# Mixer of a hybrid encoder layer: recurrences and in-projections emitted in alternation

## Chip, cores and metric

One core of a Trainium2 chip runs the whole kernel in one launch. The metric is device time in microseconds (us): the median of several executions. TensorE (PE) does the matmuls, VectorE (DVE), ScalarE (ACT) and GpSimd (POOL) the arithmetic around them, SyncE (SP) issues most DMAs.

## The reference

One layer of a streaming encoder: 2048 tokens, width 1024, float32. What the change touches is the mixer:

```python
proj = x @ w_in                                   # one in-projection
mq, mk, mv, mo, mi, mf, gq, gk, gv, gg, glr = split(proj)
mq, mk = split(silu(causal_conv(concat(mq, mk))))
hm = mlstm_chunkwise(mq, mk, mv, i_pre, f_pre)    # 4 heads, C_t = f C_{t-1} + i v k^T
m_out = sigmoid(mo) * head_layer_norm(hm)
log_a = log_sigmoid(glr @ g_lr_w + g_lr_b) / 16
hg = gla_chunked(gq, gk, gv, log_a)               # 4 heads, S_t = diag(a_t) S_{t-1} + k v^T
g_out = silu(gg) * head_rms_norm(hg)
mixed = concat(m_out, g_out) @ w_out
```

A layer norm, cross-attention into 256 memory tokens, a squared-ReLU MLP and further norms follow. Both recurrences carry a state along the tokens, so within a head one chunk needs the state of the chunk before.

## The kernel before

The mixer's work is cut into 24 units, `units` at L827: for each of the six head groups (mLSTM heads 0 and 1, GLA pairs 0 and 1, mLSTM heads 2 and 3) four token blocks of 512. A unit has two halves. The first is dense: `inproj(u)` (L831) calls `m_inproj` or `g_inproj`, which multiply the block's 1024 input features by the head's weights. Float32 precision is made from pairs of float16 values, high and low, so each product is three matmuls: `mm3`, L170 to L172. `inproj_fm` gives one group of 24 matmuls of 512 columns into one PSUM buffer of `mm` (two buffers), `inproj_tm` two groups of 48 matmuls of 256 columns in two halves each. An mLSTM unit has 48 of 512 and 96 of 256, a GLA unit 48 and 192.

The second half is the recurrence, `rec(u)` at L841. For an mLSTM unit, `m_pre` (L419) makes decay weights (`mb`, `scb`), the products of queries and keys (L433) and transposed keys (L439), and `m_rec` (L445) goes through four chunks of 128 tokens: L455 and L457 give the output, L460 the state's product, L465 on DVE the new state `C`. For a GLA unit, `g_gate` (L564) makes the cumulated gates two units ahead, and `g_rec` (L583) builds the masked product of queries and keys from seven levels of block width (64 down to 1). For each level DVE and POOL take differences of gates (L596, L597), ACT the exponential (L598), DVE and POOL multiply (L599, L600), ACT and DVE split into `lxh` and `lxl` (L603, L604), PE does 24 matmuls of 64 columns into `s` (four buffers), and DVE copies the result under a mask (L613). A diagonal (L617 to L624), the decays, transposes of the keys and four chunks (L651 to L663) follow.

The loop over units (L886 to L917) emits for each u: `g_gate(u + 2)`, `m_pre(u)`, `rec(u)`, then `inproj(u + 3)` whole (`LOOK = 3`; three in-projections stand before the loop), and in the first units parts of the cross-attention's weight products (`x_w`, `x_a`, `x_b`). A framework's scheduler then orders each engine's instructions, by the order of emission and its own estimate of when each is ready; every engine executes its own list in order. The gate arithmetic of all mLSTM heads (`gate_math`, ending at L412) stands just before the loop. After the loop the first two output tiles of the mixer, `s1(0)` and `s1(1)` (L807), multiply by `w_out`. Weights come by DMA into one staging buffer each, are scanned for their maximum (L114) and split by ACT (L147) and DVE (L148).

## Time and profile before

| | |
|---|---|
| median of 3 runs | 3002.34 us (3002.3 to 3006.09) |
| the profiled execution | 3002.87 us, its span 3001.0 us |
| TensorE's mean granted clock in it | 0.951 of full |
| busy: TensorE, VectorE, ScalarE, GpSimd | 2738.2, 1991.3, 1096.3, 447.6 us |

Times on the trace count from the span's start. The loop over units runs from about 247 us to 1200 us; what follows is the output products, the cross-attention and the MLP. A granted clock of 1.00 is 2.4 GHz, 0.50 is 1.2 GHz, and a value between is a mean over a stretch with both. A wait is listed as the engine and line that waited, an arrow, and the engine, buffer and line that ended the wait.

### The profile page before, as it was taken

The page shows a single profiled execution, that of the slowest core. Times are in us where ns is not written, and L with a number is a line of the kernel's source. Part 1 is how long each engine was busy: PE and PEld are TensorE (multiplying, and loading weights), DVE is VectorE, ACT ScalarE, POOL GpSimd, SP SyncE. Part 2 cuts the span into 40 slices and gives each one's busy share as a digit, 9 for nine tenths or more (in the row PEclk, how much of TensorE's full clock was granted, in tenths as well). Part 3 has the DMA queues.
Part 4 walks back from the last instruction along what each step waited for, and adds up shares of the span by engine and source line. Part 5 has one row for each costly group of instructions (what it writes and reads, how often), then busy time and mean ns, then how long its engine had stood idle before and what let it go on. Part 6 is the DMA issues. An engine that isn't in the chain of part 4 may idle for free.

```text
span 3001.0 us, 41124 instructions
## 1 busy us (share of the span) xinstructions
PE 2738.2 (91%) x16282; PEld 1545.8 (52%) x16282; DVE 1991.3 (66%) x3774; ACT 1096.3 (37%) x1715; POOL 447.6 (15%) x573
## 2 busy tenths in 40 slices
PE   3679989989998898999999779999999999999997
PEld 2346667666665665565565334444444444444443
DVE  8956774655768666676666467777776676555547
ACT  3335444434444543233223254444443222222230
POOL 1102113322433221121111110000000000000003
PEclk8789999988989999999999889999999999999999
DMA  7832331010001335344435963333345522122211
GB/s 240 240 118 86 106 97 38 20 42 9 23 26 62 98 120 128 66 133 106 109 102 134 175 216 142 134 134 134 134 146 141 194 90 109 67 77 78 78 53 57
DMA packets 276993, 319.51 MB, mean 106 GB/s; under 512 B 200944, under 2 KB 217856, under 8 KB 268096
## 3 DMA queue, kind: packets, MB, share of 16 engines
q1 hardware_dynamic: 268096, 285.43, 31.3%
q0 software_dynamic: 8704, 31.46, 2.9%
q8 instruction: 127, 2.08, 0.3%
q14 instruction: 66, 0.54, 0.1%
HBM read 165.58 MB, written 102.96 MB: 89 GB/s over the span
## 4 chain that ended last, share of the span: by engine, by line
PE 67%; DVE 15%; issue 7%; POOL 4%; ACT 3%; DMA 2%; SPq 2%; POOLq 0%; ACTq 0%; DVEq 0%
PE s L170 9%; PE s L171 9%; PE s L172 9%; PE mm L170 9%; PE mm L172 8%; PE mm L171 8%; PE o L172 4%; PE o L170 4%; PE o L171 4%; SPq L222 2%; DVE wmx L114 1%; DVE qk L334 1%; DVE wlo L148 1%; DVE st L199 1%; PE o L651 1%
## 5 line engine op out<-in xcount | busy, mean ns | idle before, releaser
L1245 DVE SCALAR_TENSOR_TENSOR slab<-s,uiv,slab 128x512 f32<-128x512 f32 x384 | 285.5, 748 | 99.0 <-PE s L172 97.5
L170 PE MATMUL mm<-whi,slab 128*128 128x256 f16 x1024 | 280.3, 274 | 12.4 <-ACT whi L147 7.2
L171 PEld LDWEIGHTS <-whi 128*128 128x128 f16 x1680 | 167.1, 99 | 238.8 <-issue 70.6
L171 PE MATMUL mm<-wlo,slab 128*128 128x256 f16 x1024 | 280.3, 274 | 2.7 <-DVE wlo L148 2.7
L172 PE MATMUL mm<-whi,slab 128*128 128x256 f16 x1024 | 280.3, 274 | 0.0
L172 PEld LDWEIGHTS <-wlo 128*128 128x128 f16 x1936 | 191.9, 99 | 168.4 <-issue 12.6
L170 PEld LDWEIGHTS <-whi 128*128 128x128 f16 x1680 | 167.0, 99 | 198.0 <-issue 13.8
L171 PE MATMUL s<-w,ua 128*128 128x512 f16 x512 | 194.0, 379 | 1.8 <-DVE w L148 1.8
L170 PE MATMUL s<-w,ua 128*128 128x512 f16 x512 | 194.0, 379 | 0.0
L172 PE MATMUL s<-w,ua 128*128 128x512 f16 x512 | 194.0, 379 | 0.0
L172 PE MATMUL o<-slab,wlo 128*128 128x256 f16 (+1 forms) x640 | 189.1, 295 | 0.0
L170 PE MATMUL s<-w,ub 128*128 128x512 f16 x480 | 182.6, 380 | 2.9 <-DVE r L1245 2.9
L171 PE MATMUL s<-w,ub 128*128 128x512 f16 x480 | 182.6, 380 | 0.0
L172 PE MATMUL s<-w,ub 128*128 128x512 f16 x480 | 182.4, 380 | 0.0
L170 PE MATMUL mm<-slab,whi 128*128 128x512 f16 x448 | 178.4, 398 | 0.4 <-ACT sg L343 0.4
L171 PE MATMUL mm<-slab,whi 128*128 128x512 f16 x448 | 178.4, 398 | 0.0
L172 PE MATMUL mm<-slab,wlo 128*128 128x512 f16 x448 | 178.1, 397 | 0.0
L170 PE MATMUL mm<-hf,whi 128*128 128x512 f16 x384 | 146.4, 381 | 11.5 <-ACT slab L1142 11.5
L171 PE MATMUL mm<-hf,whi 128*128 128x512 f16 x384 | 146.3, 381 | 0.0
L172 PE MATMUL mm<-hf,wlo 128*128 128x512 f16 x384 | 146.3, 381 | 0.0
L170 PEld LDWEIGHTS <-slab 128*128 128x128 f16 x1104 | 109.3, 99 | 64.8 <-issue 23.2
L170 PE MATMUL o<-slab,wlo 128*128 128x256 f16 x512 | 139.7, 273 | 0.0
(423 smaller groups left out, 6296.8 us busy)
## 6 DMA issues: line engine op xcount, KB each, us to landing
stg<-in_w_ff SPq DMA_DIRECT2D x17, 1024.0 KB
w_d<-w SPq DMA_DIRECT2D x32, 512.0 KB
slab<-in_w_ff SPq DMA_DIRECT2D x15, 1024.0 KB
w<-w_d SPq DMA_DIRECT2D x30, 512.0 KB
stg<-in_w_x SPq DMA_DIRECT2D x14, 1024.0 KB
stg<-in_w_mix SPq DMA_DIRECT2D x14, 1024.0 KB
h_d<-hs POOLq DMA_DIRECT2D x24, 512.0 KB, 3.8
x<-in_x SPq DMA_DIRECT2D x16, 512.0 KB
```

Source lines behind the costliest of these rows:

```text
L114: nc.vector.tensor_reduce(dst, src, axis=AX.X, op=ALU.max, apply_absolute_value=True)
L148: nc.vector.scalar_tensor_tensor(lo, stg, s, hi, ALU.mult, ALU.subtract)
L170: nc.tensor.matmul(psum, lhsT=lh, rhs=rh, start=(start and i == 0), stop=False)
L171: nc.tensor.matmul(psum, lhsT=lh, rhs=rl, start=False, stop=False)
L172: nc.tensor.matmul(psum, lhsT=ll, rhs=rh, start=False, stop=(stop and i == n - 1))
L199: nc.vector.bn_stats(st[:, i, :], x[:, i * 512:(i + 1) * 512])
L222: nc.sync.dma_start_transpose(dst, src)
L334: nc.vector.scalar_tensor_tensor(cv, raw[:, t:t + TB], cj[:, t:t + 1], cv, ALU.mult, ALU.add)
L651: nc.tensor.matmul(po[j][:, c], lhsT=ATb[j][:, c], rhs=vs[j][:, c], start=True, stop=(S is None))
L1245: nc.vector.scalar_tensor_tensor(acc[ii][:, ns], po, iv, acc[ii][:, ns], ALU.mult, ALU.add)
```

## The change

The functions that emit dense work (`inproj_fm`, `inproj_tm`, `m_inproj`, `g_inproj`) become generators that pause after each half group: 12 matmuls of 512 columns or 24 of 256. `m_pre`, `m_rec` and `g_rec` pause after each step: a level, the diagonal, a chunk and so on. The loop takes a step of `rec(u)`, then one half group of `inproj(u + 2)` (in the first five units also a piece of the cross-attention's products), and so on in turn. So the look-ahead is two units and no longer three; `inproj(2)` moves from before the gate arithmetic into the loop; `m_pre(u + 1)` is emitted inside `rec(u)`; a GLA level's factors are emitted two levels ahead (`prep_level`, with three `lx` buffers for four); the scaled queries are written into `q` in place; `s1(0)` and `s1(1)` are emitted in unit 22. Dense work that is left when a recurrence has ended follows it.

```diff
@@ -295,4 +295,7 @@
             hi, lo = (t.rearrange("p (k n) -> p k n", k=KC) for t in w)
-            mm3(pq, [(hi[:, k, n0:n0 + P], lo[:, k, n0:n0 + P], hT[b][:, :, 0, k, :], hT[b][:, :, 1, k, :])
-                     for k in range(KC)])
+            for k0 in (0, KC // 2):
+                mm3(pq, [(hi[:, k, n0:n0 + P], lo[:, k, n0:n0 + P], hT[b][:, :, 0, k, :], hT[b][:, :, 1, k, :])
+                         for k in range(k0, k0 + KC // 2)], k0 == 0, k0 > 0)
+                if k0 == 0:
+                    yield
             nc.scalar.activation(dst, pq, AF.Copy, scale=scale)
@@ -307,3 +310,6 @@
                         [(hT[b][:, i, 0, k, :], hT[b][:, i, 1, k, :], hi[:, k, :], lo[:, k, :]) for k in range(KC)])
+                    if v == 0:
+                        yield
                 cb(u, pv.rearrange("p (i n) -> p i n", i=2))
+                yield
 
@@ -322,3 +328,3 @@
                 raw = wk.tile([P, 3 + TB], F32, name="raw", bufs=2)
-                inproj_fm(b, (qh, ql), j * P, raw[:, 3:3 + TB], qv)
+                yield from inproj_fm(b, (qh, ql), j * P, raw[:, 3:3 + TB], qv)
                 if b == 0:
@@ -336,2 +342,3 @@
                 qk.append(cv)
+                yield
             v1 = wk.tile([P, CPB, P + 1], F32, name="v1", bufs=3)
@@ -343,3 +350,3 @@
                 nc.scalar.activation(sg[:, u * 2:u * 2 + 2, :], pv[:, :, P:2 * P], AF.Sigmoid, scale=vv)
-            inproj_tm(b, (vh, vl), cb)
+            yield from inproj_tm(b, (vh, vl), cb)
             nc.gpsimd.tensor_tensor(sg, sg, mng[:, h * P:(h + 1) * P].unsqueeze(1).broadcast_to([P, CPB, P]), ALU.mult)
@@ -429,3 +436,3 @@
                 nc.scalar.activation(mb[:, c], mb[:, c], AF.Exp, bias=gcols["c"][:, g0 + c:g0 + c + 1])
-            nc.gpsimd.tensor_tensor(scb, scb, q, ALU.mult)
+            yield
             pS = ps_s()
@@ -436,2 +443,4 @@
                                            mb.rearrange("p c t -> p (c t)"), ALU.mult, ALU.mult)
+            nc.gpsimd.tensor_tensor(q, q, scb, ALU.mult)
+            yield
             pk = ps_s()
@@ -442,3 +451,3 @@
                                     gcols["wj"][:, g0:g0 + 4].unsqueeze(2).broadcast_to([P, CPB, P]), ALU.mult)
-            mpre[u] = mb, scb, kw
+            mpre[u] = mb, q, kw
 
@@ -446,2 +455,5 @@
             q, k, v1, sg = blk
+            nxt = m_pre(u + 1) if u + 1 < len(units) and units[u + 1][0] == "m" else iter(())
+            next(nxt, None)
+            yield
             g0 = h * 16 + b * 4
@@ -467,3 +479,8 @@
                         st_m[h] = Cn
+                    if v == 0:
+                        yield
                 nc.scalar.copy(num[:, u * 2:u * 2 + 2], pn)
+                yield
+                next(nxt, None)
+                yield
             st = sm.tile([P, CPB, 6], F32, name="mst", bufs=2)
@@ -533,4 +550,6 @@
             k = wk.tile([P, TB], F32, name="qk1", bufs=3)
-            inproj_fm(b, (qh, ql), 0, q, 1.0 / QK_UP)
-            inproj_fm(b, (qh, ql), P, k, 1.0 / QK_UP)
+            yield from inproj_fm(b, (qh, ql), 0, q, 1.0 / QK_UP)
+            yield
+            yield from inproj_fm(b, (qh, ql), P, k, 1.0 / QK_UP)
+            yield
             vs = [wk.tile([P, CPB, P + 1], F32, name="v1", bufs=3)[:, :, 0:P],
@@ -546,4 +565,4 @@
                     nc.scalar.activation(zg[j][:, u * 2:u * 2 + 2, :], pv[:, :, j * P:(j + 1) * P], AF.Silu, scale=gv)
-            inproj_tm(b, (vh, vl), cbv)
-            inproj_tm(b, (gh, gl), cbg)
+            yield from inproj_tm(b, (vh, vl), cbv)
+            yield from inproj_tm(b, (gh, gl), cbg)
             mx = sm.tile([P, 2, CPB], F32, name="gmx")
@@ -587,5 +606,5 @@
             bc = bcs.pop(u)
-            for li_, m in enumerate(LEVELS):
+            def prep_level(m):
                 nb = TB // (2 * m)
-                x = p2.tile([P, TB], F32, name="lx", bufs=4)
+                x = p2.tile([P, TB], F32, name="lx", bufs=3)
                 b4 = bc.rearrange("p (n w m) -> p n w m", w=2, m=m)
@@ -604,2 +623,10 @@
                 nc.vector.tensor_tensor(xl, x, xh, ALU.subtract)
+                return xh, xl
+
+            lev = [prep_level(m) for m in LEVELS[:2]]
+            yield
+            for li_, m in enumerate(LEVELS):
+                if li_ + 2 < len(LEVELS):
+                    lev.append(prep_level(LEVELS[li_ + 2]))
+                xh, xl = lev.pop(0)
                 pl = [ps_s()[:, 0:256].rearrange("p (c t) -> p c t", c=CPB) for j in range(2)]
@@ -616,2 +643,3 @@
                         pl[j].rearrange("p c (n m) -> p (c n) m", m=m))
+                yield
             for j in range(2):
@@ -624,2 +652,3 @@
                                           pd.rearrange("p (c t) -> p c t", c=CPB))
+            yield
             e0 = rk[0].tile([P, TB], F32, name="mb")
@@ -635,2 +664,3 @@
             nc.gpsimd.tensor_tensor(kg, kg, k, ALU.mult)
+            yield
             pk = ps_s()
@@ -640,2 +670,3 @@
             nc.scalar.copy(kT, pk)
+            yield
             nums = [rk[0].tile([P, CPB, P + 1], F32, name="num", bufs=1)[:, :, 0:P], p2.tile([P, CPB, P], F32, name="num2")]
@@ -664,4 +695,9 @@
                         st_g[p] = Sn
+                    yield
                 for j in range(2):
                     nc.scalar.copy(nums[j], po[j])
+            if units[u + 1][0] == "m":
+                nxt = m_pre(u + 1)
+                for _ in nxt:
+                    yield
             junk = p2.tile([P, P], F32, name="junk")
@@ -834,3 +870,3 @@
                 wcur[kind, h] = m_weights(h) if kind == "m" else g_weights(h)
-            blks[u] = m_inproj(h, b, wcur[kind, h]) if kind == "m" else g_inproj(h, b, wcur[kind, h])
+            blks[u] = yield from (m_inproj if kind == "m" else g_inproj)(h, b, wcur[kind, h])
             nxt = u // NB * NB + NB
@@ -843,7 +879,9 @@
             if kind == "m":
-                m_rec(h, b, blks.pop(u), u)
-            else:
-                g_rec(h, b, blks.pop(u), u)
+                return m_rec(h, b, blks.pop(u), u)
+            return g_rec(h, b, blks.pop(u), u)
+
+        def run(g):
+            for _ in g:
+                pass
 
-        LOOK = 3
         x_mem()
@@ -865,3 +903,3 @@
         gates(1)
-        inproj(0)
+        run(inproj(0))
         hT += [slab([P, CPB, 2, KC, P], F16) for b in (2, 3)]
@@ -876,3 +914,4 @@
             gates(b)
-            inproj(b - 1)
+            if b == 2:
+                run(inproj(b - 1))
         gate_math()
@@ -882,23 +921,18 @@
         x_w(nx, pool=pw)
-        nu = LOOK
         gla = None
         xa = []
-        for u in range(len(units)):
-            if u + GA < len(units) and units[u + GA][0] == "g":
-                g_gate(u + GA)
-            for uu in (u, u + MA):
-                if uu < len(units) and units[uu][0] == units[u][0] == "m" and uu not in mpre:
-                    m_pre(uu)
-            rec(u)
-            if not XO and xa:
-                x_b(xa.pop())
-            if nu < len(units):
-                if units[nu][0] == "g" and gla is None:
-                    pxctx.close()
-                    gla = ExitStack()
-                    g_setup(gla.enter_context(tc.tile_pool(name="p2", bufs=1, reuse_waits="tile", side="right")))
-                inproj(nu)
-                nu += 1
-            if XO and xa:
+
+        def dense(u):
+            if u + 2 < len(units):
+                yield from inproj(u + 2)
+            if u == len(units) - 2:
+                s1(0, bw)
+                yield
+                s1(1, bw)
+                yield
+
+        def x_dense(nx):
+            if xa:
                 x_b(xa.pop())
+                yield
             if nx < 8:
@@ -906,5 +940,28 @@
                 xa.append(nx)
+                yield
+
+        run(m_pre(0))
+        for u in range(len(units)):
+            if u == 5:
+                pxctx.close()
+                gla = ExitStack()
+                g_setup(gla.enter_context(tc.tile_pool(name="p2", bufs=1, reuse_waits="tile", side="right")))
+            if u + GA < len(units) and units[u + GA][0] == "g":
+                g_gate(u + GA)
+            ds = [dense(u)]
+            if u < 5:
+                ds.append(x_dense(nx))
                 nx += 1
-                if nx < 8:
-                    x_w(nx, pool=pw)
+            r = rec(u)
+            n = 2 if u < 5 else 1
+            for _ in r:
+                for _ in range(n):
+                    while ds:
+                        if next(ds[0], 0) is None:
+                            break
+                        ds.pop(0)
+            for d in ds:
+                run(d)
+            if u < 5 and nx < 8:
+                x_w(nx, pool=pw)
             if units[u] == ("g", 1, NB - 1):
@@ -915,4 +972,2 @@
                 wqk, vo = b_x_weights()
-        s1(0, bw)
-        s1(1, bw)
```

The instruction lists of PE, DVE, POOL and SP hold as many instructions as before; ACT's has 29 table loads more (120 for 91).

In the last mLSTM heads, PE's list before has products of queries and keys, transposes and state products each as one run of four; `qk_`, `v_` and `kw` are tiles of one unit, `slab` and `whi` those of an in-projection:

```order
L433 MATMUL s<-qk_10766,qk_10802 128x128 x4
L439 MATMUL s<-ident,qk_10802 128x128 x4
L170 LDWEIGHTS whi
L170 MATMUL mm<-slab,whi 128x512
L171 LDWEIGHTS whi
L171 MATMUL mm<-slab,whi 128x512
L455 MATMUL o<-v_10808,mb 128x129 x3
L460 MATMUL s<-v_10808,kw 128x129 x4
L457 MATMUL o<-C,scb 128x129 x2
L455 MATMUL o<-v_10808,mb 128x129
```

After, at the same place, one chunk's three products stand between dense matmuls (six of 24 rows are shown on one side, five on the other):

```order
L172 LDWEIGHTS wlo
L172 MATMUL mm<-slab,wlo 128x512
L467 MATMUL o<-v_11130,mb 128x129
L469 MATMUL o<-C,qk_11067 128x129
L472 MATMUL s<-v_11130,kw 128x129
L170 LDWEIGHTS whi
L170 MATMUL mm<-slab,whi 128x512
L171 LDWEIGHTS whi
```

What moved: the next chunk's products and the four state products no longer follow one another; 12 dense matmuls stand between two chunks.

In a GLA unit, DVE's list before makes splits (`lxl`) three at a time and then mask copies of several levels (`AT`) in a run:

```order
L604 TENSOR_TENSOR lxl<-lx,lxh 128x512 x3
L613 COPY_PREDICATED AT_4088<-lmask,s 128x32x8
L613 COPY_PREDICATED AT_4089<-lmask,s 128x32x8
L613 COPY_PREDICATED AT_4088<-lmask,s 128x64x4
L613 COPY_PREDICATED AT_4089<-lmask,s 128x64x4
L613 COPY_PREDICATED AT_4088<-lmask,s 128x128x2
L613 COPY_PREDICATED AT_4089<-lmask,s 128x128x2
L604 TENSOR_TENSOR lxl<-lx,lxh 128x512
```

After, copies of one level, differences and products of levels further on and splits take turns:

```order
L615 TENSOR_TENSOR lx<-bc 128x16x16
L623 TENSOR_TENSOR lxl<-lx,lxh 128x512
L615 TENSOR_TENSOR lx<-bc 128x32x8
L618 TENSOR_TENSOR lx<-lx,qk_5616 128x16x16
L618 TENSOR_TENSOR lx<-lx,qk_5616 128x32x8
L640 COPY_PREDICATED AT_3848<-lmask,s 128x128x2
L640 COPY_PREDICATED AT_3849<-lmask,s 128x128x2
L623 TENSOR_TENSOR lxl<-lx,lxh 128x512
```

What moved: the mask copies of a level stand between the factors of later levels, and no run of several levels is left there.

In the second and third unit of the loop, before, PE's list has the second unit's chunks after its state products:

```order
L460 MATMUL s<-v_1348,kw 128x129 x4
L455 MATMUL o<-v_1348,mb 128x129
L457 MATMUL o<-C,scb 128x129
L455 MATMUL o<-v_1348,mb 128x129
L457 MATMUL o<-C,scb 128x129
L455 MATMUL o<-v_1348,mb 128x129
L433 MATMUL s<-qk_1734,qk_1770 128x128 x3
```

After, at that place, the last chunks of the second unit and the first of the third (`v_1931`) follow each other:

```order
L467 MATMUL o<-v_1348,mb 128x129
L469 MATMUL o<-C,qk_1306 128x129
L467 MATMUL o<-v_1348,mb 128x129
L469 MATMUL o<-C,qk_1306 128x129
L472 MATMUL s<-v_1348,kw 128x129
L448 MATMUL s<-ident,qk_1918 128x128 x4
L467 MATMUL o<-v_1931,mb 128x129
L469 MATMUL o<-C,qk_1875 128x129
L467 MATMUL o<-v_1931,mb 128x129 x2
L472 MATMUL s<-v_1931,kw 128x129 x2
L440 MATMUL s<-qk_2281,qk_2325 128x128
L469 MATMUL o<-C,qk_1875 128x129
```

What moved: the third unit's chunks, which before stand some 500 rows further on, directly follow those of the second, with no in-projection between.

## Rows read from the trace of the kernel before

**Rows 1.** Page, part 1: busy time, share and instructions.

```profile
PE 2738.2 (91%) x16282; PEld 1545.8 (52%) x16282; DVE 1991.3 (66%) x3774; ACT 1096.3 (37%) x1715; POOL 447.6 (15%) x573
```

**Rows 2.** Busy times by stretch; then clock, DMA share, GB/s.

```profile
247.00:400.00 153.00, 135.22 (x973) 100.25 (x972) 103.45 (x221) 68.88 (x104) 30.94 (x50) 0.97 0.28 95
400.00:558.00 158.00, 147.33 (x1068) 107.96 (x1067) 88.54 (x236) 67.10 (x100) 42.93 (x46) 0.97 0.20 64
558.00:989.00 431.00, 394.50 (x3523) 269.38 (x3522) 298.49 (x717) 190.68 (x292) 148.13 (x165) 0.87 0.10 30
989.00:1142.00 153.00, 139.11 (x961) 102.38 (x960) 98.04 (x228) 73.89 (x111) 32.20 (x49) 0.94 0.36 122
1142.00:1200.00 58.00, 43.02 (x224) 24.38 (x223) 39.73 (x95) 17.55 (x26) 11.71 (x12) 0.88 0.49 112
1200.00:3001.00 1801.00, 1726.82 (x8651) 848.21 (x8648) 1175.47 (x1966) 587.59 (x982) 151.87 (x192) 0.98 0.38 117
```

**Rows 3.** The same view: two GLA units, two 5 us pieces, one mLSTM unit.

```profile
613.50:680.90 67.40, 58.44 (x480) 40.49 (x478) 36.97 (x91) 23.03 (x38) 19.02 (x21) 0.80 0.08 25
742.80:796.10 53.30, 49.86 (x477) 34.70 (x475) 38.75 (x99) 25.49 (x39) 21.11 (x21) 0.97 0.10 32
635.00:640.00 5.00, 3.87 (x14) 2.99 (x14) 4.07 (x9) 2.72 (x4) 1.25 (x3) 0.53 0.00 0
640.00:645.00 5.00, 5.00 (x22) 3.38 (x22) 1.98 (x6) 0.81 (x2) 1.95 (x3) 0.50 0.00 0
1083.40:1108.30 24.90, 24.90 (x181) 17.93 (x180) 14.30 (x34) 10.60 (x18) 6.40 (x9) 1.00 0.32 117
```

**Rows 4.** TensorE's waits, 558 to 989: total us, times, longest.

```profile
PE s L170 <- ACT bc L574: 7.4, 5, 6.0
PE s L170 <- DVE AT L613: 6.4, 5, 2.3
...
PE o L653 <- DVE C L661: 1.3, 2, 0.9
```

**Rows 5.** TensorE's timeline: start us, us, instruction.

```profile
301.86 0.27 PE L170 MATMUL mm<-whi,slab 128*128 128x256 f16 x1 [0.64 <-ACT raw L298]
301.97 0.27 PE L171 MATMUL mm<-wlo,slab 128*128 128x256 f16 x1
```

**Rows 6.** DVE groups, 558 to 989: busy us, mean ns, idle before.

```profile
L613 DVE COPY_PREDICATED AT<-lmask,s 128x256 f32<-128x256 uint8 x112 | 50.2, 521 | 9.1 <-PE s L172 8.9
L604 DVE TENSOR_TENSOR lxl<-lx,lxh 128x512 f16<-128x512 f32 x53 | 40.0, 777 | 0.8 <-ACT lxh L603 0.7
L596 DVE TENSOR_TENSOR lx<-bc 128x256 f32<-128x256 f32 x49 | 29.5, 614 | 0.0
L599 DVE TENSOR_TENSOR lx<-lx,qk 128x256 f32<-128x256 f32 x49 | 28.2, 588 | 2.2 <-ACT lx L598 2.0
...
L148 DVE SCALAR_TENSOR_TENSOR wlo<-stg,w_s,whi 128x2048 f16<-128x2048 f32 x6 | 14.4, 2407 | 3.6 <-ACT whi L147 3.6
```

**Rows 7.** ACT groups, 558 to 989, same columns.

```profile
L598 ACT ACT_TABLE_LOAD x8 | 10.3, 1283 | 14.8 <-DVE lx L596 14.7
```

**Rows 8.** DVE's timeline, opening.

```profile
238.78 0.42 DVE L366 TENSOR_TENSOR_SCAN gm_x<-gm_c 64x128 f32<-64x128 f32 x1
```

**Rows 9.** TensorE's waits, 247 to 400.

```profile
PE mm L170 <- ACT sg L343: 7.1, 4, 2.7
PE mm L170 <- DVE xo L758: 5.1, 3, 3.2
PE s L460 <- DVE C L465: 3.2, 1, 3.2
```

**Rows 10.** TensorE's waits, 989 to 1142.

```profile
PE o L455 <- DVE mb L435: 7.7, 2, 5.5
PE o L455 <- DVE lnb L186: 5.8, 1, 5.8
```

**Rows 11.** TensorE's waits, 1142 to 1200.

```profile
PE mm L170 <- DVE r L818: 8.8, 3, 6.8
```

## What the change should do to the time

> **What bounds the kernel now.** I read the page's first part, then the busy time and granted clock of each engine over stretches of the mixer, then the two places where the clock sinks, then the waits of TensorE. TensorE is busy 91% of the span [rows 1], so only two things can shorten it: its idle time, and stretches in which it works at less than its full clock. The stretches show both [rows 2]. From 1200 us on (the output products and the FFN, which the change leaves alone) it is busy 1726.82 of 1801 us at 0.98. The mixer's loop lies between 247 and 1200. I price a stretch as idle time plus busy time x (1 - clock), the time that the lower clock adds:
> - opening, 247 to 400: 17.8 idle + 4.1 clock = 21.9 us
> - rest of the first mLSTM heads, 400 to 558: 10.7 + 4.4 = 15.1 us
> - the eight GLA recurrences, 558 to 989: 36.5 + 51.3 = 87.8 us
> - the last mLSTM heads, 989 to 1142: 13.9 + 8.3 = 22.2 us
> - the tail, 1142 to 1200: 15.0 + 5.2 = 20.2 us
>
> Together 167 us, of which the GLA stretch has more than half, most of it clock. DVE is no bound there as a mean: busy 298.49 of 431 us, 37.3 per recurrence.
>
> The next rows show how idle time and clock hang together [rows 3]. In the recurrence at 613.5 the unit takes 67.4 us at a clock of 0.80; in the one at 742.8 it takes 53.3 at 0.97. Their work at full clock is alike, 58.44 x 0.80 = 46.8 and 49.86 x 0.97 = 48.4; their idle time is 9.0 and 3.4. Inside the first, 635 to 640 has 3.87 us of work in 5, and in the next 5 us TensorE is busy throughout, but at 0.50, that is 1.2 instead of 2.4 GHz. So a stall of one or two us costs several more in the stretch behind it. The unit at 1083.4, in the last heads, has no idle time and a clock of 1.00: such a stretch exists in this kernel, when the dense matmuls stand between the steps.
>
> Who causes the stalls: TensorE waits for level factors and for mask copies (the gate cumulant 7.4 us with one of 6.0, the mask copy 6.4 in five) [rows 4], that is, for DVE and ACT chains of the recurrence, while dense in-projection matmuls that need none of it stand behind in its queue.
>
> **The change part by part.** TensorE's instructions are the same in number; nothing of its work is removed. What moves is the place of the dense matmuls. One half group is 12 matmuls of 512 columns or 24 of 256. Successive starts of 256 columns are 0.11 us apart [rows 5], so 24 x 0.11 = 2.6 us; 12 of twice the width are the same.
>
> *GLA stretch.* After the change a level is 24 small matmuls, then a half group, and its factors are made two levels ahead. The DVE work of a level is 0.61 + 0.59 + 0.78 + 2 x 0.52 = 3.0 us [rows 6], against 2.6 us of dense plus the small matmuls themselves: DVE keeps pace as a rule, and the two levels of lead, some 6 us, take up the rest. The work at full clock is 394.50 x 0.87 = 343 us. What stays idle: in the order the last two chunks of each recurrence have no dense work between them, 16 waits for the state at 1.3 / 2 = 0.65 us [rows 4] = 10 us. Six weight preparations push 2.4 us [rows 6] and a reduction of like length (an estimate from that row) into DVE's row; I let each cost 2 us beyond the lead = 12 us; and 2 us for ACT. Together 24 us, 3 per recurrence. Clock: I take 0.96, just under the 0.97 of the good unit, which has 3.4 us idle [rows 3]: 343 / 0.96 = 357, 14 more, rounded to 15 for the first recurrence. 343 + 24 + 15 = 382, a gain of **49**. Bounds: all of it comes back, 88; only idle time does, 36.5 - 24 = 12.
>
> *ACT.* Finer mixing of exponentials, Silu and sigmoid adds 29 table loads, counted in the two instruction lists; one took 1283 ns [rows 7], so 37 us of ACT. ACT is busy 190.68 of 431 us [rows 2] and makes level factors two ahead, so I take 2 us in the GLA stretch; if the lead is gone, each load stands on a level's chain, at most 37.
> By the Trainium skill's page "ScalarE: Activation LUTs", section "What ACT_TABLE_LOAD costs", a switch is the load, 1283 ns, and a drain of about 1380 ns, some 2.66 us. The load agrees with the row. By that page 29 switches would be an estimated 77 us of ACT instead of 37, and the bound of this term would double; the term itself would not move while ACT has room.
>
> *Opening.* Look-ahead falls from three to two blocks, so the in-projection of block 2 goes from before the gate arithmetic into the loop. Its transposes need the scan that DVE starts at 238.78 [rows 8]. In the order after, TensorE meets the first of these transposes some 11.5 us of dense work earlier than now, and I read up to 9 us of stall from it. The recurrences of blocks 1 and 2 then stand nearly bare, their chunks chained through the state update: eight boundaries, at 0.65 (as above) to 3.2 us, the longest such wait here [rows 9], so 5 to 26 us. Against it stand 12 us of present waits for sg and xo [rows 9] that the order shifts. Between -23 (9 + 26 - 12) and +7 I take **-5** (9 + 8 - 12). From block 4 on the order alternates cleanly: of 15.1 I take **12**. Together +7.
>
> *Last mLSTM heads.* The four state products no longer stand in one lump; between two chunks lie 12 matmuls, 2.6 us, more than the 0.65 that a state update keeps TensorE waiting. The waits of the first product of a recurrence, 7.7 us for mb and 5.8 while DVE made a layer norm's factors [rows 10], become rarer: the part before a recurrence is emitted inside the one ahead. The unit at 1083.4 shows what that looks like. I leave 6 of 22.2, gain **16** (bounds 8, 22).
>
> *Tail.* The first two output tiles move into block 22. They need only block 20 and earlier heads, so dense work covers the last two recurrences; the 8.8 us wait for r [rows 11] is paid in part elsewhere, since the two buffers of mm remain. Gain **8** (0 to 15).
>
> *At nothing:* the product with q in place instead of in scb stays on GpSimd and is needed a step later; one lx buffer less is covered by the lead of two.
>
> Sum: 7 + 49 + 16 + 8 = 80, against the profiled execution's own 3002.87 us: 2922.9; that execution lies 0.5 over the median, so **2922 us**. This case's own range, from its terms: gains of 44 to 117, 2885 to 2958.
>
> **Rivals.**
> *The clock does not come back.* TensorE's many short waits at the steps become shorter, yet stay. The evidence for it: one stall of 1.1 us in 5 [rows 3] already goes with the halved clock. Against: the unit at 742.8 has 3.4 us of idle and 0.97. Gains then 12 (GLA) + 8 + 6 + 4 = 30: **2972**.
> The Trainium skill's page "TensorE: Matmul & The Clock Gate", section "A second HAM failure mode: psum-queue depth-cycling", says that short idles between groups of matmuls can make the clock swing between its levels. By that rule the alternation, which puts a possible idle at each step, ends as this rival does; the rows bear it out only where the idle is over a microsecond.
>
> *DVE becomes the bound in GLA.* It is busy 0.69 of the stretch now. Were 0.725 all it can reach, because each level's chain passes through POOL and ACT, the stretch would take 298.49 / 0.725 = 412, a gain of 19: 80 - 30 = 50, **2952**. For: the good unit has 38.75 of 53.3, just 0.73. Against: the lead of two levels is new.
>
> *Slower: the alternation is fixed, TensorE takes its queue in order.* A recurrence has 14 steps (seven levels, diagonal, decays, transposes, four chunks). Where a step's input is late, TensorE stands, with 2.6 us of dense matmuls behind the step that it could have run; now several stand before it. The present loss is 87.8 / 8 = 11 us a recurrence, so it decides from 11 / 14 = 0.8 us of lateness a step on. At 1.5 us (between there and the 2.3 us of the longest wait for a mask copy [rows 4]) it is 21 us a recurrence, 8 x 10 = 80 lost; less 31 from the other terms it is 49 slower, **3052**. At 1.1 us all cancels. For: DVE's 3.0 us a level is more than the dense 2.6. Against: the small matmuls add to the 2.6 and the lead holds two levels.
>
> That the change does not do what it says is excluded by the order from block 4 on; in the opening it is in the term.
>
> **How the numbers follow.** My forecast 0.62, the clock stays low 0.15, DVE 0.08, late steps 0.15, of which a third cancels (within 0.2%, 6 us, about what a measurement of this kernel can tell from no change) and two thirds come out slower. So faster 0.85, same 0.05, slower 0.10. For 8 in 10 I leave out these last 0.15 and some 0.05 below: **2875 to 2980**, 10 us beyond the forecast's own lower end, and 8 above the clock rival.
>
> **What would show it.** In the profile after: GLA units of about 48 us with a clock of 0.95 or more and little idle; mLSTM units near 25 us; a stall at the gate transposes and bare recurrences in the first 150 us of the loop; ACT with 37 us more, beside other work. Were the GLA units at 0.87 with less idle, the clock rival; were DVE over 90% busy in them or TensorE's waits mostly for mask copies, the second; many waits of 1 to 2 us with dense matmuls behind each, the third. I am wrong if the gain does not lie mostly in the GLA clock.

## The result, and the profile after

The changed kernel takes 2967.03 us (median of 4 runs, 2960.39 to 2974.37) against 3004.08 for the kernel before beside it: a ratio of 0.9877, 95% interval 0.9852 to 0.9902. The forecast was 2922, so the direction holds and the size does not: 37 us gained, not 80. The profiled execution was the slowest of the four, 2974.37 us with a span of 2972.6, so between the two traces lie 28 us.

Where the difference lies is read at equal work. I count each matmul at its full-clock length and place the boundaries where the same share of that work is done: before at 236, 559, 993 and 1223 us, after at 239, 583, 993 and 1194. These are equal shares of the work and not the same matmuls (3539 and 3431 in the GLA stretch). The windows of before (columns as in [rows 2]):

```profile
236.00:559.00 323.00, 294.55 (x2120) 215.59 (x2117) 197.77 (x480) 144.63 (x219) 75.27 (x98) 0.97 0.24 79
559.00:993.00 434.00, 397.06 (x3539) 271.08 (x3538) 300.52 (x722) 194.14 (x294) 148.67 (x166) 0.87 0.10 32
993.00:1223.00 230.00, 199.74 (x1320) 140.11 (x1319) 149.34 (x342) 95.10 (x153) 44.88 (x60) 0.93 0.39 113
1223.00:3001.00 1778.00, 1705.65 (x8492) 832.73 (x8489) 1161.87 (x1940) 579.93 (x964) 150.36 (x191) 0.98 0.38 118
```

and of after:

```profile
239.00:583.00 344.00, 300.86 (x2239) 218.82 (x2238) 218.90 (x503) 155.89 (x226) 83.61 (x103) 0.95 0.23 78
583.00:993.00 410.00, 367.14 (x3431) 262.10 (x3429) 286.07 (x716) 211.53 (x310) 153.40 (x166) 0.95 0.13 41
993.00:1194.00 201.00, 190.12 (x1314) 134.26 (x1312) 129.34 (x316) 98.10 (x148) 41.74 (x57) 0.98 0.37 111
1194.00:2972.00 1778.00, 1706.18 (x8490) 832.87 (x8488) 1162.30 (x1944) 581.86 (x969) 150.12 (x191) 0.98 0.38 118
```

The GLA stretch gains 24 us and the late heads with the tail 29, but the first two stretches together lose 21 (and 3 before them); the FFN part is the same. In the GLA stretch the clock is back, 0.95 for 0.87. Its idle time is not gone: 410 - 367.14 = 43 us, against 37 before. TensorE's waits there, where [rows 4] had stood (total us, times, longest):

```profile
PE s L688 <- ACT kw L670: 15.0, 3, 5.5
PE s L170 <- DVE AT L640: 11.4, 10, 2.9
PE o L469 <- DVE C L477: 5.9, 1, 5.9
```

A few long waits have taken the place of many short ones. The first of the three for `kw`, with the two stretches of 5 us behind it:

```profile
588.00:593.00 5.00, 0.62 (x6) 0.43 (x4) 3.35 (x6) 3.12 (x5) 4.32 (x5) 1.00 0.01 2
593.00:598.00 5.00, 4.22 (x21) 2.84 (x22) 0.29 (x1) 3.92 (x5) 1.63 (x2) 0.51 0.00 0
598.00:603.00 5.00, 5.00 (x31) 3.55 (x28) 0.35 (x1) 0.84 (x2) 2.49 (x2) 0.81 0.00 0
```

After the wait TensorE runs near 1.2 GHz for one piece of 5 us and is back within the next; before, such a drop lasted up to five pieces.

Who made `kw` late? ScalarE's timeline (start us, length us, instruction, in brackets its idle time and what ended it):

```profile
583.91 1.78 ACT L617 ACTIVATE lx<-lx 128x512 f32<-128x512 f32 x3 [4.91 <-POOL lx L616]
...
589.72 1.38 ACT L617 ACTIVATE lx<-lx 128x512 f32<-128x512 f32 x2 [2.21 <-DVE lx L615]
591.12 1.28 ACT L565 ACT_TABLE_LOAD   x1
592.42 0.84 ACT L565 ACTIVATE sg<-mm,winv 128x256 f32<-128x256 f32 x2
593.15 0.58 ACT L670 COPY kw<-s 128x512 f32<-128x512 f32 x1
```

The copy stands behind the next unit's exponentials (L617) and a table load. These exponentials were late themselves: ScalarE sat idle until GpSimd's L616. GpSimd's timeline:

```profile
575.97 0.41 POOL L130 PARTITION_ALL_REDUCE amx<-wmx  x1 [5.80 <-DVE AT L640]
583.28 1.75 POOL L616 TENSOR_TENSOR lx<-bc 128x256 f32<-128x256 f32 x3 [6.89 <-issue]
```

L130 is the maximum over partitions of a weight that is being prepared. It is shown as 0.41 us, but the next instruction starts 6.9 us after its end, having waited for nothing that the profile shows. The other two waits for `kw`, at 652.74 and 813.35, follow all-reduces at 641.30 and 788.95 in the same way; behind these GpSimd's next instructions are

```profile
648.79 1.18 POOL L616 TENSOR_TENSOR lx<-bc 128x256 f32<-128x256 f32 x2 [7.08 <-issue]
796.85 1.68 POOL L715 TENSOR_TENSOR grr<-gss,mhalf 128x8 f32<-128x8 f32 x1 [7.49 <-issue]
```

The kernel before has the same pause in its trace:

```profile
770.57 0.41 POOL L130 PARTITION_ALL_REDUCE amx<-wmx  x1 [5.92 <-DVE lx L596]
778.07 0.71 POOL L600 TENSOR_TENSOR lx<-lx,qk 128x256 f32<-128x256 f32 x1 [7.09 <-issue]
```

In the opening, after, two waits of TensorE stand out:

```profile
272.44 0.80 PE L467 MATMUL o<-v,mb 128*128 128x129 f32 x2 [5.13 <-DVE mb L442]
...
299.12 1.23 PE L472 MATMUL s<-v,kw 128*128 128x129 f32 x4 [5.22 <-DVE kw L450]
```

and GpSimd, which helps to make `mb` (L434), has the same pause before the first:

```profile
253.35 0.41 POOL L130 PARTITION_ALL_REDUCE amx<-wmx  x1 [6.40 <-DVE mr L492]
260.75 1.25 POOL L434 TENSOR_TENSOR mb<-mb,cneg 128x512 f32<-128x512 f32 x1 [6.99 <-issue]
```

Behind these products, held up with them, VectorE's list comes to `mb` only at 271.70:

```profile
265.52 1.24 DVE L501 SCALAR_TENSOR_TENSOR mt<-mt,ym_s,mr 128x4 f32<-128x4 f32 x1 [6.50 <-POOL mt L500]
...
271.70 0.68 DVE L442 SCALAR_TENSOR_TENSOR mb<-s,mb 128x512 f32<-128x512 f32 x1
```

The second, for `kw`, stands right behind two reductions of weights in VectorE's list:

```profile
293.98 4.48 DVE L114 TENSOR_REDUCE wmx<-stg 128x1 f32<-128x2048 f32 x2 [1.68 <-DMA stg<-in_w_mix]
298.38 0.68 DVE L450 TENSOR_TENSOR kw<-s,gT_wj 128x512 f32<-128x512 f32 x1
```

### The profile page after: what moved, and what is told of

Same layout as the page of the kernel before. It is cut to its first block, busy times and chain, and to the rows that moved or that the text cites. A ratio compares the mean times of both kernels' runs of the same rounds, so it can differ in the third digit from the quotient of the medians.

```text
span 2972.6 us, 41072 instructions
## 1 busy us (share of the span) xinstructions
PE 2709.5 (91%) x16282; PEld 1534.7 (52%) x16282; DVE 1973.1 (66%) x3774; ACT 1131.2 (38%) x1744; POOL 454.8 (15%) x573
## 4 chain that ended last, share of the span: by engine, by line
PE 68%; DVE 15%; issue 5%; ACT 4%; POOL 3%; DMA 3%; SPq 2%; POOLq 0%; ACTq 0%; DVEq 0%
PE s L170 9%; PE mm L170 9%; PE s L171 9%; PE s L172 9%; PE mm L171 9%; PE mm L172 9%; PE o L172 4%; PE o L170 4%; PE o L171 4%; SPq L222 2%; DVE wlo L148 1%; DVE wmx L114 1%; DVE st L199 1%; DVE lxl L623 1%; ACT whi L147 1%
## 5 line engine op out<-in xcount | busy, mean ns | idle before, releaser
L170 PE MATMUL mm<-whi,slab 128*128 128x256 f16 x1024 | 287.9, 281 | 13.0 <-ACT whi L147 7.4
L171 PE MATMUL mm<-wlo,slab 128*128 128x256 f16 x1024 | 287.4, 281 | 2.7 <-DVE wlo L148 2.7
L172 PE MATMUL mm<-whi,slab 128*128 128x256 f16 x1024 | 287.5, 281 | 0.0
L170 PEld LDWEIGHTS <-whi 128*128 128x128 f16 x1680 | 166.4, 99 | 205.8 <-issue 17.4
L170 PE MATMUL s<-w,ua 128*128 128x512 f16 x512 | 194.8, 380 | 0.6 <-ACT w L147 0.6
L170 PE MATMUL s<-w,ub 128*128 128x512 f16 x480 | 182.6, 380 | 2.9 <-DVE r L1300 2.9
L170 PE MATMUL mm<-slab,whi 128*128 128x512 f16 x448 | 173.3, 387 | 4.5 <-DVE xo L794 3.9
L171 PE MATMUL mm<-slab,whi 128*128 128x512 f16 x448 | 172.8, 386 | 0.0
L170 PE MATMUL mm<-hf,whi 128*128 128x512 f16 x384 | 146.5, 381 | 12.5 <-ACT slab L1197 12.5
L170 PEld LDWEIGHTS <-slab 128*128 128x128 f16 x1104 | 111.7, 101 | 67.3 <-issue 24.2
L170 PE MATMUL o<-slab,wlo 128*128 128x256 f16 x512 | 140.0, 273 | 0.1
```

The costliest lines, as they stand in the source:

```text
L170: nc.tensor.matmul(psum, lhsT=lh, rhs=rh, start=(start and i == 0), stop=False)
L171: nc.tensor.matmul(psum, lhsT=lh, rhs=rl, start=False, stop=False)
L172: nc.tensor.matmul(psum, lhsT=ll, rhs=rh, start=False, stop=(stop and i == n - 1))
```

## The experiments

All edits are on the changed kernel unless said. e5, e10, e12 and e13 leave out the maximum across partitions for some weights, so they do not compute the layer; they show what the all-reduce costs. Line numbers are those of each run's own kernel: L170, L469 and L640 of the changed kernel are L175, L474 and L645 in e5, e12 and e13. In the table: the median, the ratio to the kernel before with its 95% interval, and from the trace the length of the three stretches of equal work (the first two of the forecast in one; GLA; late heads and tail). e6 has 42 matmuls more and no entry there.

| kernel | median us | ratio, interval | opening to 558 | GLA | late, tail |
|---|---|---|---|---|---|
| before | 3004.08 | | 323.0 | 433.9 | 230.1 |
| changed | 2967.03 | 0.9877 (0.9852 to 0.9902) | 344.2 | 409.8 | 200.6 |
| e1 opening as before | 2952.77 | 0.9850 (0.9826 to 0.9873) | 329.5 | 411.0 | 199.0 |
| e2 before, look-ahead 2 | 3013.34 | 1.0045 (1.0023 to 1.0066) | 338.7 | 438.5 | 216.0 |
| e3 copy on VectorE | 2975.61 | 0.9918 (0.9895 to 0.9941) | 340.7 | 401.3 | 212.7 |
| e4 GLA whole | 2994.73 | 0.9982 (0.9964 to 0.9999) | 350.1 | 422.2 | 206.5 |
| e5 no all-reduce, units 5 to 15 | 2951.84 | 0.9842 (0.9817 to 0.9867) | 337.2 | 394.2 | 202.1 |
| e6 e1, maximum on TensorE | 3023.70 | 1.0082 (1.0060 to 1.0103) | | | |
| e7 no lead | 2984.18 | 0.9954 (0.9936 to 0.9971) | 344.1 | 409.2 | 215.1 |
| e8 late heads whole | 2976.65 | 0.9932 (0.9908 to 0.9957) | 341.1 | 407.8 | 211.4 |
| e9 e1, one early all-reduce | 2941.18 | 0.9822 (0.9799 to 0.9846) | 335.9 | 387.5 | 200.0 |
| e10 before, no all-reduce | 2981.20 | 0.9947 (0.9929 to 0.9964) | 322.8 | 435.7 | 215.8 |
| e11 changed again | 2967.05 | 0.9914 (0.9892 to 0.9935) | 340.5 | 409.9 | 200.1 |
| e12 no all-reduce, to unit 4 | 2942.95 | 0.9815 (0.9795 to 0.9834) | 316.3 | 407.8 | 199.7 |
| e13 no all-reduce, to unit 15 | 2928.52 | 0.9775 (0.9751 to 0.9799) | 310.5 | 403.3 | 199.5 |

The kernel before moved between 2984 and 3010 us from run to run, so 10 us between two kernels of different chips decide nothing; the stretches, from one trace each, repeat within 4 us for the changed kernel (e11). An edit also moves what it does not name, as the scheduler then orders all lists anew; e3 and e7 shift the late heads by 12 and 14 us in that way.

**e1, the opening as before.**

```diff
-            if b == 2:
-                run(inproj(b - 1))
+            run(inproj(b - 1))
...
+            if u < 3:
+                run(rec(u))
+                run(inproj(u + 3))
+                run(x_dense(nx))
...
+                continue
```

> The changed kernel with the first three units of the loop as before: block 2's in-projection stands before the gate arithmetic again, recurrences 0 to 2 are emitted whole and followed by the in-projection three blocks on; alternation starts with unit 3. At equal matmul work done the changed kernel is 27 us behind the kernel before by the end of its first 90 us of loop. Theory: bare recurrences there wait behind weight preparations on VectorE; then this kernel takes 2967 - 25 = about 2942 us and the gaps of 5 us at mb and kw near 272 and 299 us are gone. Rival: the loss sits with the cross-attention's pieces that lie in the same stretch, whose waits for kh and xo also appear; then it stays at 2960 to 2970.

15 of the 21 lost us come back, and the two waits of 5 us are gone; 329.5 is still 6.5 over before, with one wait of 6.9 us for `sg` among what is left.

**e2, the look-ahead alone.** `LOOK = 2` for 3 in the kernel before, `inproj(2)` in the loop.

> The kernel before with one edit: look-ahead two units instead of three (block 2's in-projection leaves the place before the gate arithmetic), recurrences and in-projections whole, one after the other. If the opening's loss comes from the look-ahead alone, the opening loses about 25 us and nothing is won elsewhere: about 3028. If it comes from emitting in alternation, this stays near 3003 in the opening; later stretches may still lose some, since a whole recurrence then has one in-projection less to fill it.

The opening loses 16 us without any alternation, three quarters of the changed kernel's 21: most of the loss comes with the shorter look-ahead. The longest single wait of TensorE there is put down to an all-reduce; the kernel before has no such wait in its opening:

```profile
PE o L455 <- POOL amx L130: 5.4, 1, 5.4
```

**e3, the copy of `kw` on VectorE.**

```diff
-            nc.scalar.copy(kT, pk)
+            nc.vector.tensor_copy(kT, pk)
```

> The changed kernel with one edit: the copy of the transposed keys of a GLA block (kw, line 670) runs on VectorE instead of ScalarE. Three waits of TensorE for this copy cost 15.0 us, each with the next block's exponentials and a table load ahead of the copy in ScalarE's list. Theory: the copy's place in that list is the cost; then 2967 - 12 = about 2955, and the gaps before L688 fall under 1.5 us. Rival: the step is late anyway (decays and transposes come late), the wait moves to VectorE's copy; then within 3 us of 2967.

Neither expectation came. The three waits stay with 10.7 us for 15.0, now for VectorE's copy, since VectorE too stands behind the late levels. The GLA stretch gains 8.5 us, the late heads lose 12, and the median is 9 over that of the changed kernel: the copy's place in ScalarE's list is at most a small part of the three waits.

**e4, GLA recurrences whole.** `if units[u][0] == "g": run(r)` before the loop over the steps.

> The changed kernel with one edit: for the eight GLA units the recurrence is emitted whole and the in-projection two blocks on behind it; level factors two ahead and everything else stay. If the alternation is what brings the GLA stretch from 434 to 410 us and its clock from 0.87 to 0.95, this kernel loses it: about 2990, clock 0.87 to 0.90 there. If the factors made two ahead bring it, it stays near 2967.

Twelve of the 24 us of the GLA stretch go, its clock is 0.89, and alternation is half of the GLA gain in the trace. The rest comes with the other edits of the order; which, stays open. The kernel as a whole loses almost all its gain, but the other half of that lies in the opening and the late heads, 6 us each, where the program is that of the changed kernel.

**e5, no all-reduce in the GLA stretch.**

```diff
+        if own_max[0]:
+            nc.vector.tensor_copy(r, mx)
+            return r
         nc.gpsimd.partition_all_reduce(r, mx, P, bass_isa.ReduceOp.absmax)
```

> The changed kernel with one part left out: for the weights prepared from unit 5 to unit 15 the maximum across partitions (GpSimd's all-reduce, line 130) is replaced by a VectorE copy of each partition's own maximum. In the changed kernel GpSimd starts nothing for 7 us after such an all-reduce (at 576.0 and 641.3 the next level difference starts 6.9 and 7.1 us later), while ScalarE and VectorE stand idle behind it; the two waits of 5.2 and 5.5 us before L688 follow, at 593.8 and 652.7. Theory: these 7 us are the cause of the long waits in the GLA stretch; then they fall under 2 us, the clock there rises from 0.95 to 0.97, and the time is 2967 - 20 = about 2947. Rival: the waits are ScalarE's list alone (table loads and the next unit's exponentials); then 2960 to 2970.

The waits for `kw` are gone altogether, and the GLA stretch takes 394 us, 16 less, at a clock of 0.96 (0.97 expected). Its idle time is 395 - 365.50 = 29 us for 43:

```profile
578.00:973.00 395.00, 365.50 (x3435) 261.15 (x3434) 277.25 (x720) 206.68 (x306) 145.89 (x153) 0.96 0.14 45
```

The longest waits there now:

```profile
PE s L175 <- DVE AT L645: 15.2, 13, 4.9
PE o L474 <- DVE C L482: 5.3, 1, 5.3
PE mm L175 <- ACT v L566: 2.6, 2, 2.0
```

More than half of what is left are waits for VectorE's mask copies, the sign that the forecast gave for its VectorE rival.

**e6, the maximum on TensorE.** A transpose of the column, VectorE's maximum of the row, and a product that spreads it.

> The kernel with the opening as before (2952.8 us), and from unit 3 on the maximum across partitions made by TensorE and VectorE (transpose, reduction of one row, a product with ones) instead of GpSimd's all-reduce; the whole computation is kept. If GpSimd's 7 us behind each all-reduce cause the long GLA waits: 2953 - 20 = about 2933. If TensorE, which takes its list in order, now waits for VectorE's reductions of the weights instead (2.3 us each, eight of them): no gain, 2950 to 2965.

Worse than the rival asked: 71 us slower than e1. TensorE takes its list in order and now stands in it for VectorE's reductions of weights. Over the whole kernel these waits come to 39 us; where the rest of the 71 lies was not followed:

```profile
PE s L134 <- DVE wmx L114: 39.3, 7, 12.3
```

**e7, no lead.** Each level's factors are emitted right before it.

> The changed kernel with one edit: a GLA level's factors are emitted right before the level, not two levels ahead; alternation stays, and so do three buffers. If the lead of two is needed, each level waits for its chain through VectorE, GpSimd and ScalarE, about 4 us against 3.3 us of matmuls in between: the GLA stretch goes from 410 back to 430 or more, 2985 to 3000. If the scheduler moves the factors ahead by itself, as far as the buffers let it, 2960 to 2972.

The GLA stretch is unchanged (409.2): the scheduler moves the factors ahead by itself (some 630 of VectorE's 716 instructions there keep their order). The 14 us that the late heads lose were in neither expectation; the emitted order of a stretch can shift the one behind it by as much.

**e8, the late heads whole.** `if u >= 16: run(r)`.

> The changed kernel with one edit: from unit 16 on the recurrences are emitted whole and the in-projections (and the first two output tiles) behind them. By the forecast's terms the late mLSTM stretch and the tail gained 16 and 8 by alternation; at equal work done they gained 19 and 9. If alternation brought it, this kernel takes 2967 + 15 to 28 = 2982 to 2995; if it is the part before a recurrence, emitted inside the one ahead, it stays near 2967.

Of the 29 us there 11 go, between the two expectations. As e2, e3, e7 and e10 put the same stretch at 213 to 216 by edits elsewhere, it is not shown that alternation is what gave them.

**e10, the kernel before without the all-reduces.**

> The kernel before with one part left out: the maximum across partitions of the weights prepared from unit 4 to 15 of the loop is replaced by a VectorE copy of each partition's own maximum, as in the fifth run for the changed kernel. There it brought the GLA stretch from 410 to about 388 us. If the all-reduce costs the kernel before as much, about 2978 and a GLA stretch of 410; if whole recurrences with three in-projections ahead hide it, 2996 to 3004.

The time is that of the first expectation, the place is not: the GLA stretch does not move (435.7; and e5 brought it to 394, not 388), so there the pause is hidden or its place is taken by other waits. The gain, 14 us in the median, lies in the late heads. Two of the all-reduces left out stand there, the second of them just before the wait of 5.5 us for `mb` of [rows 10]:

```profile
1044.13 0.41 POOL L130 PARTITION_ALL_REDUCE amx<-wmx  x1 [5.89 <-issue]
1052.18 1.05 POOL L483 TENSOR_TENSOR mt<-mt,mhalf 128x4 f32<-128x4 f32 x1 [7.65 <-issue]
```

That wait is gone in e10, though the order changed there too (some 280 of VectorE's 342 instructions keep theirs). So the pause probably had a price in the kernel before as well; in its GLA stretch leaving it out gave nothing.

**e11, the changed kernel again.**

> The changed kernel unaltered, on the same chip as the two runs beside it, as the yardstick for differences of ten us: about 2967, ratio to the kernel before about 0.988. Its trace should show the same three waits before L688 in the GLA stretch, 15 us together.

The median and the three waits for `kw`, 15.0 us, are as expected. The ratio is not, 0.9914, as the kernel before was faster beside this run: the gain is 0.9 to 1.2%.

**e12, no all-reduce in the opening.** As e5, for weights from the head of the loop to unit 4.

> The changed kernel with one part left out: for the weights prepared from the head of the loop to unit 4 (the cross-attention's, and the first GLA pair's) the maximum across partitions and the same of the keys' product is replaced by a VectorE copy of each partition's own. In the changed kernel the wait of 5.1 us for mb at 272 us follows an all-reduce at 253.4, behind which GpSimd starts L434 only at 260.8; the wait of 5.2 us for kw at 299 follows two weight reductions on VectorE (4.5 us). If GpSimd's pause behind the all-reduce is what the bare recurrences of the opening wait for: the opening loses 10 instead of 24 us, about 2953. If it is VectorE's reductions and the shorter look-ahead: the mb wait goes, the rest stays, 2960 to 2968.

28 us in the opening (24 against e11), which is now faster than before by 6.7. I had expected at most half. The waits for `mb` and `kw` are both gone, while VectorE's reductions of the weights are still there. But the scheduler has put the opening in another order: of VectorE's 502 instructions there some 270 keep theirs, and the reductions no longer stand right before `kw`. How much the pause gives back and how much the order was not separated. The GLA stretch, whose all-reduces stay, is the control: its order is the same, and the three waits for `kw` stay:

```profile
PE s L693 <- ACT kw L675: 15.2, 3, 5.6
```

**e13, both left out.**

> The changed kernel with the maximum across partitions left out for all weights prepared from the head of the loop to unit 15 (VectorE copies each partition's own): the fifth and the twelfth run in one. If GpSimd's pause behind the all-reduces is the one cause of both misses, opening and GLA stretch, the two gains add: 2967 - 24 - 15 = about 2928, the forecast's 2922 within a few us, with an opening as fast as before's and a GLA stretch of 388 to 394. If the two overlap (what one removes the other's stretch loses again), 2938 to 2945.

2928.5, where the sum of the two says 2928. The distribution is not as expected: the opening gains 34 us by it, the GLA stretch 6.5 (403.3, not 388 to 394). The three waits for `kw` are gone here too. The 9 us over e5 are mostly clock, 0.94 for 0.96; the mask copies make TensorE wait no longer (14.9 us in 12, there 15.2 in 13). Why the clock is lower stays open.

```profile
551.50:954.80 403.30, 371.25 (x3429) 263.47 (x3427) 277.08 (x722) 206.75 (x307) 146.43 (x152) 0.94 0.14 45
```

**e9, one early all-reduce for seven weights.** A version that computes everything: e1's opening, and the maxima of the second GLA pair and the last two mLSTM heads from extra loads in units 4 to 6, reduced at once.

```diff
+            if u in (4, 5, 6):
...
+                for j in {4: (0, 1, 2), 5: (3, 4), 6: (5, 6)}[u]:
+                    absmax(mxs[:, j:j + 1], load_stage(a["w_mix"][early[j]]))
+                if u == 6:
+                    nc.gpsimd.partition_all_reduce(maxima[:, 0:7], mxs[:, 0:7], P, bass_isa.ReduceOp.absmax)
```

> The kernel with the opening as before (2952.8 us), and the maxima of the seven weights of the second GLA pair and the last two mLSTM heads taken early: three extra loads with a reduction on VectorE in unit 4, two in unit 5, two in unit 6, and one all-reduce on GpSimd for all seven columns, before the first GLA recurrence. The computation is whole. Theory: the seven single all-reduces, each with 7 us of GpSimd behind it, are what was left of idle time in the GLA stretch; then no wait at L688 above 2 us and 2953 - 20 = about 2933. Rival: the extra loads and reductions (seven times 2.3 us of VectorE) hold up units 4 to 7 as much as they save: 2950 to 2965.

2941, the fastest kernel here that computes the layer: 26 us under the changed one and 12 under e1, where the theory had 20. The GLA stretch falls to 387.5, with one wait for `kw` of 2.6 us left; 6 us go back into the opening, where the extra loads are.

## Why the prediction was wrong

**What held.** The reading that idle time and halved clock are what can be won, and that dense work between the steps wins it, is borne out: the clock of the GLA stretch is 0.95 (0.96 forecast), its clock loss 367.14 x 0.05 = 18 us (15 forecast) for 397.06 x 0.13 = 52 before. So the gain does lie mostly in the GLA clock, the sign that I had set for being right. The late heads run as the good unit of [rows 3] did, at 1.00 with 1.5 us idle in 136; with the tail they gain 29 us, 24 forecast. That this sum came out is partly luck: e2 and e10, which do not alternate, gain 14 us in the same place, and e10 does it by leaving out all-reduces. The stall at the gate transposes was feared at 9 us and is 2.06. VectorE is busy 286 of 410 us, a share of 0.70; that the stretch came out near the 412 us of the VectorE rival is chance, as most of its idle time over the forecast goes with the all-reduces (e5). Late steps came, a few by much and not each by a little, and the balance stayed a gain. The time came nearest to the rival of the clock, 2972, but not by its mechanism: the clock came back, idle time stayed.

**What failed, GLA.** The step is "What stays idle": 24 us, of which 12 for six weight preparations, priced by VectorE's rows alone. It measured 43. A preparation has a third part that I counted at nothing, the all-reduce on GpSimd, which by its row is 0.41 us and in truth keeps GpSimd from its level products for some 13 (below). A lead of two levels, 6 us, does not cover that: three all-reduces are followed by the three waits for `kw`, 15.0 us. With the all-reduces left out (e5) these waits are gone, the idle time is 29 us, and the stretch gains 40 us of the 49.

**What failed, opening.** The terms were -5 for 247 to 400 and +12 for 400 to 558; together they measured -21. I had looked for the loss in the chain of state updates and at the gates. The loss goes with the all-reduces of the cross-attention's weights: without them (e12) the two stretches gain 6.7 us. That 7 was the sum of the two terms is chance, as the order changed too. In the trace the chain from the pause to a wait can be read for `mb` at 272, not for `kw` at 299. With the look-ahead of three, before, the opening did not pay this; e1, which gives it back, and e2, which takes it from the kernel before, show 15 and 16 us of it.

**What failed, ScalarE.** Two us for 29 more table loads was no large error: loads did stand before `kw` in each of the three waits, yet with the pause gone (e5) the waits went too, loads and all. What they cost by themselves was not tried. The dearer switch that the prediction cites, with an estimate of 77 us for the 29, is not seen: in 87 of the 119 switches of the changed kernel's trace that lie between two instructions the next one starts 1.30 to 1.40 us after the one before has ended, which is the load and no more.

All in all leaving out the all-reduces (e13) brings back 38.5 us of a miss of 45 by the medians, 43 of 51 by the traces. That the all-reduces are the cause of most of the miss is shown. That they act through GpSimd's pause is shown for the three waits for `kw` in the GLA stretch; in the opening it is argued, since leaving them out also changes the order. How much falls in which stretch is not settled, since e5 and e13 differ by 9 us in the GLA stretch.

The range was too narrow for its own terms. Their bounds add up to gains of 9 (-23 + 12 + 12 + 8 + 0) to 144, and I put on record 44 to 117; the 37 measured lie inside the first and outside the second.

The rows for it were there. In the kernel before, GpSimd's idle time before L600 has 14.1 us ended by "issue", that is by nothing the profile shows, and I had read GpSimd's busy time only:

```profile
L600 POOL TENSOR_TENSOR lx<-lx,qk 128x256 f32<-128x256 f32 x49 | 44.9, 927 | 58.5 <-ACT lx L598 44.1 <-issue 14.1
```

## What to carry to other kernels

Price a step that is moved on every engine it touches, by the time from the end of the instruction before it to the start of the one behind it on that engine, not by its busy time; idle time that ends with "issue" on an engine with free inputs is a cost that some instruction leaves behind. Interleaving takes the slack out of an order: a pause that cost the GLA stretch nothing before (e10) becomes its longest wait. Look for it before the change on all engines that feed the steps, and gather rare, costly instructions into one (e9) rather than move them to an engine that takes its list in order (e6).

## What the runs showed of the hardware

An all-reduce over partitions on GpSimd costs far more than its row. Around the one at 575.97, GpSimd's sequencer has instructions that the page counts as not busy (rows of the view by line: duration in ns, first and last start):

```profile
L130 POOLq MODIFY_POOL_CONFIG  x2: 8/8/8, 570.4 to 570.4; - x2
L130 POOL PARTITION_ALL_REDUCE amx<-wmx x1: 409/409/409, 576.0 to 576.0; - x1
```

```profile
L616 POOLq MODIFY_POOL_CONFIG  x2: 83/83/83, 576.3 to 576.4; - x2
L616 POOL TENSOR_TENSOR lx<-bc x2: 602/602/603, 583.3 to 583.9; 128x256 f32<-128x256 f32 x2
```

5.6 us pass between the first pair and the all-reduce, 6.9 between the second pair and the next product: 570.4 to 583.3, 12.9 us without GpSimd for 0.41 us of work. The profile puts the way in down to a wait for VectorE's mask copy, but the all-reduce's input had been there since 566.58:

```profile
564.30 2.28 DVE L114 TENSOR_REDUCE wmx<-stg 128x1 f32<-128x2048 f32 x1
```

In the changed kernel the seven all-reduces from 575.97 to 955.01 all have 5.7 to 6.3 us before them and 6.8 to 7.5 us behind. The Trainium skill's page "GPSIMD Engine Reference", section "2.1 Instruction dispatch", says that the first call to a freshly loaded kernel pays some 6 us of code loading, measured after such an instruction, with no visible row. The trace agrees for the way in, 5.6 us, though here it is paid again at each of these calls; and it shows as much again, 6.9 us, on the way back to ordinary products. Where all-reduces stand together, as at 306.4, 306.7 and 307.0 in the changed kernel, only the last has the pause behind it. The one reduction of seven columns in e9 pays once, too:

```profile
496.97 0.41 POOL L973 PARTITION_ALL_REDUCE inv_m<-mxs  x1 [6.29 <-DVE yh L520]
504.28 2.49 POOL L580 TENSOR_TENSOR sg<-sg,gng 128x512 f32<-128x512 f32 x2 [6.90 <-ACT bc L602]
```

The way back belongs to the next product and not to the all-reduce's end: behind the pair at 274.21 copies start at once, and the pause lies 17 us further on, before the first product.

```profile
274.21 0.82 POOL L130 PARTITION_ALL_REDUCE amx<-wmx  x2 [6.20 <-issue]
274.90 0.25 POOL L335 COPY halo<-raw 128x3 f32<-128x3 f32 x1
...
291.98 0.10 POOL L346 MEMSET v<- 128x4 f32 x1 [11.10 <-PE s L472]
299.19 1.26 POOL L352 TENSOR_TENSOR sg<-sg,mng 128x512 f32<-128x512 f32 x1 [7.11 <-issue]
```

The second surprise is the clock. The GLA stretch has more idle time after (43 us for 37) and yet 0.95 for 0.87. Of pieces of 5 us, 27 of 87 had a clock under 0.90 before, 12 of 82 after. Before, these are 11 drops of one to five pieces; after, 6 drops of one to three. So the drops are half as many, and each a little shorter: the idle time after lies in fewer and longer waits. That the number of stalls, more than their sum, sets what the clock costs is what these rows suggest; no run here isolated it.
